# The first layer's gate in block form, the value weights' sums behind it, the turns of the next x ahead of other work

## The chip, the cores and the metric

One core of one Trainium2 chip runs the whole program. The metric is the time of one execution in microseconds (us), as the device reports it; the kernel before was run three times. A profiled execution gives start and duration of every instruction on the core's engines: TensorE (PE, with its weight loads PEld), VectorE (DVE), ScalarE (ACT), GpSimd (POOL), and the DMA queues that SyncE (SP) and POOL issue. A few matmul records are missing from a trace.

## The reference

Two layers over 512 tokens of width 1024. Each layer has a token mixer (layer 0 a Mamba-2 SSD, layer 1 an HGRN2), a squared-ReLU MLP, two layer norms, and at its end a gated per-layer input, which is what the change is about:

```python
for i in range(DEPTH):
    ...
    h = layer_norm(DEEPNORM_ALPHA * x + mix, ln_g[i, 0], ln_b[i, 0])
    h = layer_norm(DEEPNORM_ALPHA * h + sq_relu_mlp(h, mlp_w1[i], mlp_w2[i]), ln_g[i, 1], ln_b[i, 1])
    x = h + jax.nn.sigmoid(h @ ple_w_gate[i]) * (p[i] @ ple_w_proj[i])
```

`h @ ple_w_gate` is 512x1024 by 1024x1024, `p @ ple_w_proj` is 512x256 by 256x1024. After layer 0 the new x enters layer 1's mixer, whose value and output-gate projections (`v`, `g`) come first in this kernel.

## The kernel before

**Precision.** Every matmul operand is float32, split in two float32r parts, hi and lo. `mm3` (lines 119 to 122) makes one product of three matmuls: hi by hi, hi by lo, lo by hi, each 128x128 weights by 512 columns. A weight tile of 128x1024 comes by DMA into `raw` (3 buffers), ACT copies it to `whi` (line 113, 6 buffers) and DVE subtracts to make `wlo` (line 116). A new `whi` waits until PE has finished with the buffer that it takes over.

**Order.** On each engine the instructions stand in a fixed order. A scheduler makes it from the code and from priorities: work under a higher `high_priority` offset (SOON 40, EARLY 60, LEAD 100) is placed ahead of work that the code has earlier. Only in the stretches under `manual_schedule`, which begin with `values4`, does PE follow the code's own order. Each engine works through its list in order; an instruction that waits holds all behind it.

**Block form.** A product of two 2x2 block matrices may be made with seven block products in place of eight, with sums of blocks taken beforehand. `block_product` does this for the MLP, `values4` for the first value projections, `last_gate` for half of layer 1's gate. The sums of weight blocks are either made by DVE in tiles `r` (`weight_sums`, lines 322 to 345: eight loads on POOL's queue and eight subtractions or additions of 128x1024), or by DMAs that add to what lies there (`last_gate`, lines 399 to 408: a chain of eight on POOL's queue).

**Layer 0's gate before** (lines 616 to 670) is direct: for each half h of the 1024 columns and each chunk c of 128 tokens, eight `mm3` over the full depth into one PSUM bank, a sigmoid on ACT, then on DVE a product with the projection (line 664) and an addition to `acc` (line 666). While the gate runs, `transpose_split` (line 231) still turns h for its own input (PE transposes, line 238). Then `turn(h, c)` (line 620) turns each finished piece of the next x: four PE transposes into the bank `pt` (line 625), two ACT copies (lines 628, 629) and a DVE subtraction (line 630). The last turn is called in `values4` between its first and second product (lines 711, 712).

**values4** (line 672) makes layer 1's first value projections in block form from x and from the untransposed copies in `rows`. Its DVE sums of weights (`t1` to `t4`, tiles `r`) are loaded and added as early as the `r` tiles come free, which is during the last MLP product and the gate. Its products come in this order: two with plain weights, then with `t3`, `t2`, `t4`, `t1`, then one more with plain weights.

**Layer 1's gate before** is `last_gate` (line 397): 7 quarter products of 12 matmuls and 4 half products (`rest`, line 442) of 24, with `final` (line 449) doing sigmoid, product, addition and the store of the output.

Of the kernel before, what the change touches and what calls it, by code (L numbers as in the profile page):

```python
# [44 lines left out]
def trunk(ctx: ExitStack, tc, a):  # L45
# [180 lines left out]
    turned_last = []  # L226

# [57 lines left out]
    def norm(i, keep=None):  # L285
# [36 lines left out]
    def weight_sums(w, lead, after=None, queue=nc.gpsimd):  # L322
# [5 lines left out]
        def load(i, u, src):  # L328
            queue.dma_start(t[i][u], src)  # L329
# [67 lines left out]
    def last_gate(wp, wg, h_s, p_s, kept, turned):  # L397

        t3, t1, t2, t4 = (tmp("r", [P, 1024]) for _ in range(4))
        with tc.high_priority(offset=SOON):  # L400
# [7 lines left out]
            nc.gpsimd.dma_start(t4, wg[1], accum_op=ALU.add)  # L408

        pairs = [mk(b8, [P, 2, 4, 256], "b8", F32R) for _ in range(2)]  # L410
        cells = [mk(b8, [P, 4, T], "b8") for _ in range(3)] + [tmp("blk", [P, 4, T])]
        cell = lambda n: cells[n // 4][:, n % 4, :]
# [36 lines left out]
        def final(c, h, g, pp, pin=None):  # L449
# [3 lines left out]
            for ps, cs in pp:  # L453
# [5 lines left out]
                nc.sync.dma_start(a["out"][tok(c), fs], acc[:, c, fs])  # L459
# [30 lines left out]
        def put(n, f):  # L490
            t, ks = pairs[n // 2], slice(2 * (n % 2), 2 * (n % 2) + 2)
            ins = nc.scalar.copy(t[:, 0, ks, :], f)
            nc.vector.tensor_sub(t[:, 1, ks, :], f, f32(t[:, 0, ks, :]))
            return ins

        with tc.high_priority(offset=LEAD):
# [4 lines left out]
            pin = put(1, a11)  # L501
# [4 lines left out]
        raw = mk(raws, [P, 1024], "raw")  # L506
        pu = mk(w4, [P, 1024], "a", F32R), mk(w4, [P, 1024], "b", F32R)
        with tc.high_priority(offset=LEAD):
            nc.sync.dma_start(raw, wp[1])
            nc.scalar.copy(pu[0], raw)  # L510
            nc.vector.tensor_sub(pu[1], raw, f32(pu[0]))
        for n, c in enumerate((2, 3, 0)):
            ps = bank(psj, "pj")
            proj(ps, c, pu)
            nc.scalar.copy(cell(10 + n), ps)
# [11 lines left out]
        for u in range(2):  # L527
# [3 lines left out]
            final(2 + u, 0, cell(6 + u), [(cell(2 + u), whole)])  # L531
        for u in range(2):
# [25 lines left out]
    def mlp_and_gate(layer, h_s, last):  # L558
# [36 lines left out]
        for g, period in enumerate(PERIODS):  # L595
            if g < 4:
                tiles = hidden(g)
            if g > 0:
                if g == 4:
                    kept = tmp("blk", [P, 2, 4, 256]) if last else None  # L600
# [12 lines left out]
        if last:  # L613
            return last_gate(a[f"wp_{layer}"], a[f"wg_{layer}"], h_s, p_s, kept, turned)

        x_n = Split(8)
        rows = [tmp("blk", [P, 2, 4, 256]) for _ in range(2)]
        late = []

        def turn(h, c):  # L620

            sl = slice(c * P, (c + 1) * P)
            pt = bank(pst, "pt")
            for j in range(4):
                nc.tensor.transpose(pt[:, j * P : (j + 1) * P], acc[:, c, h * 512 + j * P : h * 512 + (j + 1) * P], ident)
            v = pt.rearrange("p (j t) -> p j t", j=4)
            hh = x_n.hi[h][:, :, sl]
            nc.scalar.copy(hh, v)
            nc.scalar.copy(rows[c // 2][:, h, :, c % 2 * P : (c % 2 + 1) * P], v)
            nc.vector.tensor_sub(x_n.lo[h][:, :, sl], v, f32(hh))  # L630

        pps = {}

        def proj(c, pu):

            ps = pps[c] = bank(*((psj, "pj") if c > 1 and pps else (psy, "py%d" % (c % 2))))
            sl = slice(c * P, (c + 1) * P)
            for k in range(2):
                ks = slice(k * 512, (k + 1) * 512)
                mm3(ps, p_s[0][:, k, sl], p_s[1][:, k, sl], pu[0][:, ks], pu[1][:, ks], k == 0, k == 1)  # L640

# [30 lines left out]
    def values4(xs, rows, late):  # L672
# [38 lines left out]
        for f in late:  # L711
            f()
# [751 lines left out]
```

## Time and profile before

| what | value |
|---|---|
| three runs | 1412.86, 1413.53, 1413.72 us (median 1413.53) |
| the profiled execution's own time | 1411.34 us |
| its span, first to last instruction | 1409.6 us |
| instructions | 20400 |
| DVE, ACT, POOL busy | 1069.1, 763.6, 45.8 us |
| layer 0's gate on PE | from about 699 us |
| the last turn of the next x on PE | 765.83 us |
| layer 1's gate on PE | from about 1350 us to the end |

Busy time of PE counts a matmul until its end is modelled to come, so that consecutive matmuls overlap: each 128x512 one is shown with 0.39 us, and the next starts 0.23 us after it. What PE loses must therefore be looked for in the gaps between starts and in the view of waits, not in the busy share.

### The profile page before, as it was taken

The page shows a single profiled execution, that of the slowest core. Times are in us where ns is not written, and L with a number is a line of the kernel's source. Part 1 is how long each engine was busy: PE and PEld are TensorE (multiplying, and loading weights), DVE is VectorE, ACT ScalarE, POOL GpSimd, SP SyncE. Part 2 cuts the span into 40 slices and gives each one's busy share as a digit, 9 for nine tenths or more (in the row PEclk, how much of TensorE's full clock was granted, in tenths as well). Part 3 has the DMA queues.
Part 4 walks back from the last instruction along what each step waited for, and adds up shares of the span by engine and source line. Part 5 has one row for each costly group of instructions (what it writes and reads, how often), then busy time and mean ns, then how long its engine had stood idle before and what let it go on. Part 6 is the DMA issues. An engine that isn't in the chain of part 4 may idle for free.

```text
span 1409.6 us, 20400 instructions
## 1 busy us (share of the span) xinstructions
PE 1404.3 (100%) x8001; PEld 1168.1 (83%) x8001; DVE 1069.1 (76%) x1778; ACT 763.6 (54%) x1156; POOL 45.8 (3%) x92
## 2 busy tenths in 40 slices
PE   9999999999999999999999999999999999999998
PEld 7888888888988888888888888888898888888887
DVE  7989688698977668677986577678785867667795
ACT  7766465573354444545555547655555454544573
POOL 0000000001000000000000000000100000000100
PEclk9999999999999999999999999999999999999999
DMA  8433333234433444345621421222443444444731
GB/s 313 135 117 120 106 120 110 85 100 156 141 113 127 157 131 152 129 142 178 209 90 49 134 91 61 76 87 96 150 135 105 147 137 148 144 137 159 202 106 60
DMA packets 50399, 181.69 MB, mean 129 GB/s; under 512 B 5632, under 2 KB 6400, under 8 KB 50176
## 3 DMA queue, kind: packets, MB, share of 16 engines
q1 hardware_dynamic: 38784, 138.45, 29.6%
q0 software_dynamic: 11520, 41.95, 9.2%
q8 instruction: 63, 1.03, 0.3%
q14 instruction: 32, 0.26, 0.1%
HBM read 177.16 MB, written 2.16 MB: 127 GB/s over the span
## 4 chain that ended last, share of the span: by engine, by line
PE 99%; DMA 0%; DVE 0%; issue 0%; DVEq 0%
PE pj L120 25%; PE pj L121 25%; PE pj L122 25%; PE py L120 5%; PE py L122 5%; PE py L121 5%; PE py L906 1%; PE pt L238 1%; PE py L1175 1%; PE pm L923 1%; PE pm L871 1%; PE py L1301 1%; PE pt L859 0%; PE py L1303 0%; PE py L1240 0%; PE py L832 0%
## 5 line engine op out<-in xcount | busy, mean ns | idle before, releaser
L113 ACT CAST whi<-raw 128x1024 fp32r<-128x1024 f32 x218 | 228.8, 1050 | 333.2 <-PE pj L121 243.6
L120 PE MATMUL pj<-b,whi 128*128 128x512 f32 (+1 forms) x990 | 378.6, 383 | 0.0
L122 PE MATMUL pj<-b,wlo 128*128 128x512 f32 (+1 forms) x990 | 376.8, 381 | 0.0
L121 PE MATMUL pj<-b,whi 128*128 128x512 f32 (+1 forms) x990 | 376.6, 381 | 0.0
L116 DVE TENSOR_TENSOR wlo<-raw,whi 128x1024 fp32r<-128x1024 f32 x218 | 265.4, 1221 | 129.4 <-ACT whi L113 128.2
L121 PEld LDWEIGHTS pj<-b,whi 128*128 128x128 f32 x990 | 186.4, 188 | 34.6 <-issue 0.9
L122 PEld LDWEIGHTS pj<-b,wlo 128*128 128x128 f32 x990 | 186.3, 188 | 34.5
L120 PEld LDWEIGHTS pj<-b,whi 128*128 128x128 f32 x990 | 186.1, 188 | 34.0
L122 PE MATMUL pj<-whi,b 128*128 128x512 f32 x520 | 204.1, 392 | 0.0
L120 PE MATMUL pj<-whi,b 128*128 128x512 f32 x508 | 202.1, 398 | 0.0
L121 PE MATMUL pj<-wlo,b 128*128 128x512 f32 x508 | 199.2, 392 | 0.0
L113 ACT CAST whi<-r 128x1024 fp32r<-128x1024 f32 x76 | 80.0, 1053 | 68.5 <-PE pj L122 39.4
L122 PEld LDWEIGHTS pj<-whi,b 128*128 128x128 f32 x520 | 97.7, 188 | 20.1
L120 PEld LDWEIGHTS pj<-whi,b 128*128 128x128 f32 x508 | 95.5, 188 | 19.1 <-ACT b L1322 0.3
L121 PEld LDWEIGHTS pj<-wlo,b 128*128 128x128 f32 x508 | 95.5, 188 | 18.7 <-issue 0.2
L116 DVE TENSOR_TENSOR wlo<-r,whi 128x1024 fp32r<-128x1024 f32 x76 | 92.5, 1220 | 19.6 <-ACT whi L113 19.1
L122 PE MATMUL py<-whi,b 128*128 128x512 f32 x260 | 101.3, 390 | 0.0
L121 PE MATMUL py<-wlo,b 128*128 128x512 f32 x248 | 96.6, 389 | 0.0
L120 PE MATMUL py<-whi,b 128*128 128x512 f32 x248 | 96.4, 390 | 0.0
L329 POOL DMA_DIRECT2D r<-in_w x64 | 34.0, 532 | 1098.8 <-DVE wlo L116 544.3
L122 PEld LDWEIGHTS py<-whi,b 128*128 128x128 f32 x260 | 48.8, 188 | 10.2
L800 DVE SCALAR_TENSOR_TENSOR cv<-pj,cst,cv 128x509 f32<-128x509 f32 (+2 forms) x66 | 48.9, 746 | 10.6 <-ACT cv L797 9.8
(368 smaller groups left out, 1943.5 us busy)
## 6 DMA issues: line engine op xcount, KB each, us to landing
raw<-in_w SPq DMA_DIRECT2D x112, 512.0 KB, 3.3
r<-in_w POOLq DMA_DIRECT2D x64, 512.0 KB, 3.8
raw<-in_wssd SPq DMA_DIRECT2D x36, 512.0 KB, 3.9
a<-csd SPq DMA_DIRECT2D x16, 512.0 KB, 4.1
raw<-in_wso SPq DMA_DIRECT2D x16, 512.0 KB, 3.3
raw<-in_whq SPq DMA_DIRECT2D x16, 512.0 KB, 3.4
raw<-in_wg SPq DMA_DIRECT2D x15, 512.0 KB, 4.0
raw<-in_whvg SPq DMA_DIRECT2D x14, 512.0 KB, 3.4
```

What stands on the lines that cost most here:

```text
L113: nc.scalar.copy(hi[:, :n], f)
L116: nc.vector.tensor_sub(lo[:, :n], f, f32(hi[:, :n]))
L120: nc.tensor.matmul(out, sh, mh, start=start, stop=False, **kw)
L121: nc.tensor.matmul(out, sh, ml, start=False, stop=False, **kw)
L122: return nc.tensor.matmul(out, sl, mh, start=False, stop=stop, **kw)
L238: nc.tensor.transpose(pt[:, j * P : (j + 1) * P], src[:, k * P : (k + 1) * P], ident)
L329: queue.dma_start(t[i][u], src)
L800: nc.vector.scalar_tensor_tensor(cv[:, d:], ps[:, : T - d], convw[:, i, k : k + 1], cv[:, d:], ALU.mult, ALU.add)
L871: nc.tensor.matmul(pst_[:, c * P : (c + 1) * P], btok[:, c, :], xw[:, c].rearrange("p h q -> p (h q)"), start=True, stop=True)
L906: mm = nc.tensor.matmul(yds[0][64 * r : 64 * r + 64, sl], xdt[:, 2 * c + r, :], m[:, r, sl], start=True, stop=True)
L923: mm = nc.tensor.matmul(yo[:, c * P : (c + 1) * P], pv[:, c - 1].rearrange("p h q -> p (h q)"), cm[:, c * P : (c + 1) * P], start=True, st ...
L1175: nc.tensor.matmul(pcs[r][bs, at : at + n], kk[r][:, ts], qs, start=True, stop=True)
```

## The change

Layer 0's gate takes the form of layer 1's. `last_gate` becomes `block_gate` with a flag `last`, and the direct form, its `proj` and its `turn` are gone. For layer 0 the block form differs from layer 1's in these points:

- the projections of the second half (`wp[1]`) are made next to the chunk that uses them, not early;
- there are fewer SBUF tiles for partial results (`cells`, `homes`), and nothing is stored to the output;
- `turn` is called at eight places, two of them (`turn(1, 0)` and `turn(1, 1)`) inside `values4`: one before the second chunk of its first product, one after that product;
- `turn` has its ACT and DVE work under LEAD, and takes the bank `pm` for even chunks and `pt` for odd ones;
- the loads of `weight_sums` for the values are placed behind the last DMA of the gate's chain (`added`) on POOL's queue, its DVE sums behind the gate's last sum of h (`summed_last`) in DVE's list.

Besides, the layer norm ahead of layer 0's gate has the priority SOON for its last two chunks too (before 0), and h keeps an untransposed copy (`kept`) in layer 0 as in layer 1.

```diff
@@ norm
-            with tc.high_priority(offset=LEAD if c == 3 and i % 2 == 0 else 0 if c > 1 and i == 1 else SOON):
+            with tc.high_priority(offset=LEAD if c == 3 and i % 2 == 0 else SOON):
@@ weight_sums
-    def weight_sums(w, lead, after=None, queue=nc.gpsimd):
+    def weight_sums(w, lead, after=None, held=None):
         def load(i, u, src):
-            queue.dma_start(t[i][u], src)
+            with behind(held):
+                nc.gpsimd.dma_start(t[i][u], src)
@@ last_gate, now block_gate
-            nc.gpsimd.dma_start(t4, wg[1], accum_op=ALU.add)
+            added = nc.gpsimd.dma_start(t4, wg[1], accum_op=ALU.add)
+        if last:
+            cells = [mk(b8, [P, 4, T], "b8") for _ in range(3)] + [tmp("blk", [P, 4, T])]
+            cell = lambda n: cells[n // 4][:, n % 4, :]
+        else:
+            cells = [mk(b8, [P, 4, T], "b8"), tmp("blk", [P, 4, T])]
+            homes = [(0, 0), (0, 1), (0, 2), (0, 3), (1, 0), (1, 1), (0, 0), (0, 1), (1, 2), (1, 3)]
+            cell = lambda n: cells[homes[n][0]][:, homes[n][1], :]
-            put(3, a12)
+            summed_last = put(3, a12)[1]
+        gate_last[:] = summed_last, added
...
+        x_n = Split(0)
+        rows = [None, None]
+        def turn(h, c):
...
+            pt = bank(pst, "pt") if c % 2 else bank(psm, "pm")
+            for j in range(4):
+                nc.tensor.transpose(pt[:, j * P : (j + 1) * P], acc[:, c, h * 512 + j * P : h * 512 + (j + 1) * P], ident)
...
+            with tc.high_priority(offset=LEAD):
+                nc.scalar.copy(hh, v)
+                nc.scalar.copy(rows[c // 2][:, h, :, c % 2 * P : (c % 2 + 1) * P], v)
+                nc.vector.tensor_sub(x_n.lo[h][:, :, tok(c)], v, f32(hh))
         for u in range(2):
+            if not last and u:
+                turn(0, 2)
             part(x[u], summed(2), t1, u, False)
             nc.vector.tensor_add(cell(8 + u), x[u], cell(8 + u))
         us = [negated(wg[6]), negated(wg[7])]
         b22 = unit(wg[5])
+        if not last:
+            pu = unit(wp[1])
+            for u in range(2):
+                g = bank(psj, "pj")
+                rest(g, 2 + u, us, True)
+                nc.vector.tensor_add(cell(8 + u), g, cell(8 + u))
+                ps = bank(psj, "pj")
+                proj(ps, 2 + u, pu)
+                final(2 + u, 1, cell(8 + u), [(ps, whole)])
+                if u == 0:
+                    turn(0, 3)
+            for u in range(2):
+                part(x[u], summed(3), b22, u, False, False)
+                if u:
+                    turn(0, 1)
+                rest(x[u], u, us, False)
+                if u == 0:
+                    turn(0, 0)
+                ps = bank(psj, "pj")
+                proj(ps, u, pu)
+                final(u, 1, x[u], [(ps, whole)])
+                turn(1, 2 + u)
+            return x_n, rows, [lambda: turn(1, 0), lambda: turn(1, 1)]
@@ mlp_and_gate: the direct form goes
-        if last:
-            return last_gate(a[f"wp_{layer}"], a[f"wg_{layer}"], h_s, p_s, kept, turned)
...
-                for k in range(8):
-                    ks = slice((k % 2) * 512, (k % 2 + 1) * 512)
-                    mm3(pg, h_s.h(k, sl), h_s.l(k, sl), gu[k // 2][0][:, ks], gu[k // 2][1][:, ks], k == 0, k == 7)
...
+        return block_gate(a[f"wp_{layer}"], a[f"wg_{layer}"], h_s, p_s, kept, turned, last)
@@ values4
-        t1, t2, t3, t4 = weight_sums(w, VALUE_SUMS)
+        t1, t2, t3, t4 = weight_sums(w, VALUE_SUMS, *gate_last)
         def product(x, us, banks, start, drain):
             for c in range(2):
+                if late and c:
+                    late.pop(0)()
         product(part(0, 0), [unit(v) for v in w[0][0]], x, True, first(0, 0))
-        for f in late:
-            f()
+        late.pop(0)()
         product(part(0, 1), [unit(v) for v in w[1][0]], z, True, more(0, 0))
```

How the lists of the engines move, at three places. A row names the line, the operation, the tile written and the tiles read, the size, and the engines or DMA queues that it waits for.

**The eight sums of the value weights on DVE.** Before, they stand during the last MLP product and the first half of the gate; the last four of them (tiles `r`, lines 339 to 344) stand among the gate's own products and additions (lines 664, 666) and the splits of h (line 243):

```order
L339 TENSOR_TENSOR r_6348<-r_6348,r_6344 128x1024 [waits DMASW5_49]
L664 TENSOR_TENSOR sg_5966<-py_1021_5923,sg_5966 128x512 [waits Activation_49]
L243 TENSOR_TENSOR b_921_5529<-pt_5992,b_919_5527 128x4x128 [waits Activation_49]
L666 TENSOR_TENSOR acc_99<-sg_5966,acc_99 128x512 [waits DVE_49]
L340 TENSOR_TENSOR r_6344<-r_6342,r_6344 128x1024
L243 TENSOR_TENSOR b_920_5528<-pt_6019,b_918_5526 128x4x128 [waits Activation_49]
L344 TENSOR_TENSOR r_6345<-r_6345,r_6343 128x1024 [waits DMASW6_49]
```

Now six of the eight stand in the last third of the gate, where line 573 adds a half product, line 463 multiplies by the projection, line 465 adds to `acc` and line 559 is the subtraction of a turn:

```order
L573 TENSOR_TENSOR blk_5904<-pj_6262,blk_5904 128x512 [waits PE_49]
L342 TENSOR_TENSOR r_6384<-r_6382,r_6384 128x1024
L463 TENSOR_TENSOR sg_6283<-pj_6276,sg_6283 128x512 [waits PE_49,Activation_49]
L338 TENSOR_TENSOR r_6383<-r_6383,r_6389 128x1024 [waits DMASW4_49,DMASW3_49]
L465 TENSOR_TENSOR acc_99<-sg_6283,acc_99 128x512 [waits DVE_49]
L341 TENSOR_TENSOR r_6389<-r_6389,r_6385 128x1024 [waits DMASW5_49,DVE_49]
L346 TENSOR_TENSOR r_6386<-r_6386,r_6384 128x1024 [waits DMASW6_49]
L342 TENSOR_TENSOR r_6385<-r_6383,r_6385 128x1024 [waits DVE_49]
L559 TENSOR_TENSOR b_1053_6188<-pm_6306,b_1052_6187 128x4x128 [waits PE_49,Activation_49]
L346 TENSOR_TENSOR r_6387<-r_6387,r_6385 128x1024 [waits DMASW7_49,DVE_49]
L463 TENSOR_TENSOR sg_6321<-pj_6314,sg_6321 128x512 [waits PE_49]
```

The sums have moved from ahead of and beside the gate's first half to just ahead of the last chunks' additions to `acc`.

**The last addition to acc ahead of the last turn, on DVE.** Before, it is line 666 on `sg_6303`, and it stands ahead of the two weight splits (line 116) of tiles `r_6343` and `r_6344`, the sum t2:

```order
L664 TENSOR_TENSOR sg_6303<-py_1069_6295,sg_6303 128x512 [waits Activation_49]
L630 TENSOR_TENSOR b_1003_5890<-pt_6331,b_1001_5888 128x4x128 [waits PE_49,Activation_49]
L666 TENSOR_TENSOR acc_99<-sg_6303,acc_99 128x512 [waits DVE_49]
L1016 CAST lmask_6658<-raw_6659 128x256 [waits DMAHW0_49]
L116 TENSOR_TENSOR wlo_6507<-r_6343,whi_6505 128x1024 [waits Activation_49]
L116 TENSOR_TENSOR wlo_6511<-r_6344,whi_6509 128x1024 [waits PE_49,Activation_49]
L630 TENSOR_TENSOR b_1003_5890<-pt_6417,b_1001_5888 128x4x128 [waits PE_49,Activation_49]
```

Now it is line 465 on `sg_6368`, and it stands behind the same two splits (tiles `r_6384`, `r_6385`), its product (line 463) and a sum of x (line 712):

```order
L116 TENSOR_TENSOR wlo_6556<-r_6384,whi_6554 128x1024 [waits Activation_49]
L116 TENSOR_TENSOR wlo_6560<-r_6385,whi_6558 128x1024 [waits Activation_49]
L463 TENSOR_TENSOR sg_6368<-pj_6361,sg_6368 128x512
L712 TENSOR_TENSOR blk_6189<-blk_6189 128x1024
L465 TENSOR_TENSOR acc_99<-sg_6368,acc_99 128x512 [waits DVE_49]
L713 TENSOR_TENSOR blk_6189<-blk_6189,blk_6305 128x1024 [waits DVE_49]
L1014 CAST lmask_6707<-raw_6708 128x256 [waits DMAHW7_49]
L679 TENSOR_TENSOR b_1119_6514<-blk_6189,b_1119_6514 128x1024 [waits Activation_49]
L559 TENSOR_TENSOR b_1080_6326<-pt_6466,b_1079_6325 128x4x128 [waits PE_49,Activation_49]
```

The addition that the last turn reads has passed from ahead of the splits of t2 to behind them.

**The last turn on PE.** It stands at the same place as before, after the last matmul of `values4`'s first product; now with these rows:

```order
L121 MATMUL py_1099_6411<-wlo_6430,b_1052_6187 128x512
L122 MATMUL py_1099_6411<-whi_6428,b_1053_6188 128x512
L553 MATMUL pt_6466<-cst_165,acc_99 128x128 [waits DVE_49,PE_49]
L553 MATMUL pt_6466<-cst_165,acc_99 128x128 x3
L120 MATMUL pj_6412<-whi_6476,b_1079_6325 128x512 [waits Activation_49]
```

`whi_6558`, which the second split on DVE reads, takes over the buffer of `whi_6428`; the matmul of the second row here is the last one that uses it.

More of the change, by code (lines that the diff above doesn't have):

```diff
@@ L226, in trunk @@
     turned_last = []
+    gate_last = []
     def behind(ins):
@@ L599, in mlp_and_gate @@
                 if g == 4:
-                    kept = tmp("blk", [P, 2, 4, 256]) if last else None
+                    kept = tmp("blk", [P, 2, 4, 256])
                     h_s, after, turned, sums = norm(2 * layer + 1, kept)
```

86 lines of the change are left out of this document (23 added, 63 removed).

## The prediction

> **What bounds the kernel now.** I read the page first, then the view of PE's waits, then the busy time by stage. The page:
>
> ```profile
> span 1409.6 us, 20400 instructions
> PE 1404.3 (100%) x8001; PEld 1168.1 (83%) x8001; DVE 1069.1 (76%) x1778; ACT 763.6 (54%) x1156; POOL 45.8 (3%) x92
> PE 99%; DMA 0%; DVE 0%; issue 0%; DVEq 0%
> ```
>
> The chain that ended last is PE for 99% of the span. Whether PE ever stood still is told by its waits over the whole execution:
>
> ```profile
> PE pm L153 <- PEq L1452: 0.8, 1, 0.8
> PE py L749 <- DVE b L167: 0.6, 1, 0.6
> ```
>
> There are two, both in the first microseconds, 1.4 us together. So the program lasts as long as PE's list of matmuls, and a change can act in two ways only: by the number of matmuls, or by a wait that PE does not have now. Which engine could make PE wait around layer 0's gate is seen by stage (columns: stretch, then busy us of PE, PEld, DVE, ACT, POOL with instructions, granted clock, DMA share, GB/s; the fourth is in layer 1's gate, which already has the block form):
>
> ```profile
> 699.00:727.00 28.00, 28.00 (x143) 23.12 (x142) 25.62 (x39) 14.63 (x28) 0.00 (x0) 1.00 0.20 67
> 727.00:757.00 30.00, 30.00 (x141) 24.80 (x140) 16.72 (x21) 13.23 (x19) 0.00 (x0) 1.00 0.22 71
> 757.00:772.00 15.00, 15.00 (x71) 12.17 (x70) 12.44 (x14) 9.87 (x14) 0.00 (x0) 1.00 0.35 115
> 1355.00:1376.00 21.00, 21.00 (x103) 17.30 (x102) 20.29 (x28) 16.63 (x30) 0.00 (x0) 1.00 0.20 67
> ```
>
> The reader is to see that DVE is nearly full at the start of either gate (25.6 of 28 us, 20.3 of 21 us), and has room from 727 to 757 us (16.7 of 30). That room is where the change puts more work. The third view is the timeline around the last turn of the next x, where PE meets what DVE made last. Its rows give all durations that I need:
>
> ```profile
> 763.42 0.69 DVE L666 TENSOR_TENSOR acc<-sg,acc 128x512 f32<-128x512 f32 x1
> ...
> 765.60 0.39 PE L122 MATMUL py<-whi,b 128*128 128x512 f32 x1
> 765.83 0.60 PE L625 MATMUL pt<-cst,acc 128*128 128x128 f32 x4
> 766.19 0.48 PE L120 MATMUL pj<-whi,b 128*128 128x512 f32 x1
> 766.50 0.40 PE L121 MATMUL pj<-wlo,b 128*128 128x512 f32 x1
> 766.51 1.05 ACT L113 CAST whi<-r 128x1024 fp32r<-128x1024 f32 x1
> ...
> 767.60 1.23 DVE L116 TENSOR_TENSOR wlo<-r,whi 128x1024 fp32r<-128x1024 f32 x1 [0.58 <-ACT whi L113]
> 768.74 0.69 DVE L630 TENSOR_TENSOR b<-pt,b 128x512 fp32r<-128x512 f32 x1
> 769.34 0.68 DVE L702 TENSOR_TENSOR a<-pj,a 128x512 f32<-128x512 f32 x1
> 769.94 1.22 DVE L714 TENSOR_TENSOR blk<-blk 128x1024 f32<-128x1024 f32 x1
> 770.17 0.39 PE L122 MATMUL pj<-whi,b 128*128 128x512 f32 x1
> 770.39 0.39 PE L120 MATMUL pj<-whi,b 128*128 128x512 f32 x1
> 770.59 1.06 ACT L113 CAST whi<-r 128x1024 fp32r<-128x1024 f32 x1 [2.06 <-PE pj L122]
> 771.19 1.23 DVE L715 TENSOR_TENSOR blk<-blk,blk 128x1024 f32<-128x1024 f32 x1
> ```
>
> A matmul starts 0.23 us after the one ahead (770.17, 770.39) and ends 0.39 us after its start. Four transposes cost 0.36 us and make the next gap 0.31 instead of 0.23: 0.44 in all. An ACT copy of a weight tile that waits for its buffer starts 0.03 us after the end of the last matmul on it (770.17 + 0.39, 770.59) and takes 1.05. DVE's split follows 0.04 us later (766.51 + 1.05, 767.60). On a busy DVE, one row of 1024 columns puts the next 1.14 us later (767.60, 768.74), one of 512 columns 0.60 (768.74, 769.34); a single result is ready after 1.22 or 0.69. And the addition to `acc` that the last turn reads was ready at 764.11, 1.7 us ahead of the turn at 765.83. That is the margin today.
>
> **The change part by part.**
>
> *Fewer matmuls.* The direct gate is 2 halves x 4 chunks x 8 mm3 = 64 mm3, 192 matmuls. The block form is 7 quarter products of 4 mm3 and 4 half products of 8 mm3 = 60 mm3, 180 matmuls. Projections (16 mm3) and turns (8 x 4 transposes) are as many as before. 12 matmuls fewer x 0.227 us = **-2.7 us**, and that is all that can be gained.
>
> *The sums of the gate's weights by DMA.* Eight more DMAs on POOL's queue, in a chain where each addition waits for what it adds to, and the values' loads now stand behind them there. Layer 1's gate shows the same chain and its last user, and the present loads and sums of the values stand in the view of the tiles r from 650 to 730 us:
>
> ```profile
> 1304.75 0.53 POOL L401 DMA_DIRECT2D r<-in_wg  x1 [20.86 <-DVE wlo L116]
> 1333.24 0.86 POOL L408 DMA_DIRECT2D r<-in_wg  x1 [5.57 <-DMA r<-r]
> 1372.57 1.22 DVE L116 TENSOR_TENSOR wlo<-r,whi 128x1024 fp32r<-128x1024 f32 x1
> ```
>
> ```profile
> L329 POOL DMA_DIRECT2D r<-in_whvg x8: 527/530/537, 653.4 to 675.0; - x8
> L336 DVE TENSOR_TENSOR r<-r,r x2: 1220/1220/1220, 680.5 to 681.6; 128x1024 f32<-128x1024 f32 x2
> L344 DVE TENSOR_TENSOR r<-r,r x2: 1218/1221/1224, 718.5 to 721.5; 128x1024 f32<-128x1024 f32 x2
> DMA to landing us min/median/max: 3.6/3.8/4.8
> ```
>
> The gates lie about 651 us apart (first gate load here at 1304.75, first value load at 653.4, both when the same r tile comes free), so in layer 0 the chain runs from about 653 to 682 us. Four of the eight values' loads then find tiles free; the others wait for the gate's own splits, the last at 1372.57 - 651 = 721 us, and land within 5 us, by 727. The sums that need them stand far back in DVE's list and run after about 742 us (below), so these loads cost **0**; were the 15 us of cover gone, each late load would hold DVE for up to 4.8 us.
>
> *More on DVE.* In the order, from the last half product added to `acc`'s second half (line 573) to the row ahead of t2's splits, DVE has 22 rows: 12 of 1024 columns, six of them value sums, and 10 of 512. That is 12 x 1.14 + 10 x 0.60 = 19.7 us. In the same stretch PE has 78 matmuls and five turns, 78 x 0.227 + 5 x 0.44 = 19.9 us. The two run level: DVE has neither margin nor a large debt when PE reaches the last turn. I take **0.3 us** of debt; the ends are 0 and 1.2 (one wide row).
>
> *The last turn waits for what cannot be made earlier.* This is the term that decides. PE's last turn reads `acc` after the addition of line 465, which on DVE stands behind both splits of t2. The second split reads `whi_6558`, whose ACT copy waits for the last matmul on `whi_6428`, and this matmul is the one directly ahead of the turn on PE. So PE stands still for the whole loop. Without a wait the turn would come at 765.83 - 2.72 = 763.1, the matmul ahead of it starting at 762.9. Step by step: its end, 763.27; ACT copy from 763.30 to 764.35; split on DVE from 764.39; its product (line 463) at 765.53; the wide sum (line 712) at 766.13; the addition (line 465) from 767.27 to 767.96; the turn, with a weight load of its own, at about 768.1. **+5.0 us**, in place of the present margin of 1.7. Everything behind the turn on PE's list is moved by it. Queued behind the addition on DVE are line 713, a small cast, the split of line 679 (which needs ACT's copy, 1.05 us, after line 713) and then the turn's own subtraction, which the third matmul of the second product's second chunk needs: 767.9 + 1.22 + 1.05 + 1.14 + 0.69 = 772.0 against 768.1 + 0.44 + 12 x 0.227 + 0.45 = 771.7, with the weight load **+0.5 us** (ends 0 and 1).
>
> *The other turns.* Six turns in the gate wait for additions to `acc` in the same way, but with no loop through PE; counted along DVE's list they come within half a microsecond of their need. I take **+0.1**, ends 0 and 1. The ACT copies of `kept` and of the cells (some 20 of about 0.6 us) lie in ACT's idle time: 13.2 of 30 us are used. Elsewhere in the program the lists are the same but for names.
>
> The sum: -2.7 + 5.0 + 0.3 + 0.5 + 0.1 = **+3.2 us**. Against the profiled execution that is 1409.6 + 3.2 = 1412.8 us of span, with 1.7 us around it as now (1411.34 - 1409.6) 1414.5. The median of the runs lies 2.2 us above that execution: 1413.53 + 3.2 = **1416.7 us**. With the ends of the terms the forecast's own range is -2.7 + 5.0 = +2.3 to -2.7 + 5.0 + 1.2 + 1 + 1 = +5.5: 1415.8 to 1419.0.
>
> **The rivals.**
>
> *PE's clock falls in the wait.* The granted clock is 1.00 in every row above, but PE nowhere stands still for more than 0.8 us, so the trace cannot show what 5 us do. After the 0.6 us wait of line 749 the next matmuls follow at the usual spacing. If the clock fell, the product behind the turn, 24 matmuls of 0.227 = 5.4 us, would be slower in part; all of it at half speed is the upper end, +5.4, a quarter of it +1.4. I take +1.4: 1418.1.
> [...]
>
> *The wait is not there, or short: not slower.* If the buffer of `whi_6558` came free before the first product ends, or the addition were ready while DVE still has margin, the turn would meet its rows as it does today, and only the 12 matmuls would count, with the 0.5 behind: 1413.53 - 2.7 + 0.5 = 1411.3. It decides as soon as the addition is ready by 763. For it: the margin today is 1.7 us with the same splits nearby. Against it: today's addition stands ahead of those splits, and the rows at 766.51 and 770.59 show ACT copying right behind PE's last use.
>
> *DVE falls behind earlier.* If its 1024-column rows run later than counted, say because a raw weight tile lands late, the turns of the gate's last third wait too, each for 0.3 to 0.6 us, four of them, +2: 1418.7. For it: DVE and PE run level there. Against: layer 1's gate keeps PE without a wait with DVE busy in 20.3 of 21 us.
>
> **How the numbers follow.** Forecast 0.5, the clock 0.2, the short wait 0.2, DVE behind 0.1. A measurement of this kernel can tell about 0.2%, 2.8 us, from no change: faster is below 1410.7, slower above 1416.4. The forecast lies just above that bound, so of its 0.5 about 0.35 are slower and 0.15 same; the clock and the late DVE are slower (0.3); of the short wait 0.04 are faster, 0.16 same. Together: slower 0.65, same 0.31, faster 0.04. The range reaches over the clock's case and below the forecast's own low end, 1414.0 to 1419.2; most of the short wait's chance is left out below.
>
> **What would show it.** In the profile of the changed kernel: 12 matmuls fewer; one wait of PE at line 553 on DVE (line 465) of about 5 us, at about 763 us, and one of about half a microsecond behind it; ACT's copy directly behind the last matmul ahead of the wait, then DVE without a gap until line 465. Wrong would be: no such wait, waits spread over several turns, a DMA as the releaser, or a clock below 1.00 behind the wait.

## The result, and the profile after

The changed kernel takes 1421.04 us (median of 6 runs, 1418.69 to 1422.47) against 1412.92 us of the kernel before (6 runs, 1411.61 to 1413.72): ratio 1.0056, 95% interval 1.0043 to 1.0069, or 6.1 to 9.7 us more. It is slower, as predicted, but by 8.1 us where 3.2 were forecast, and outside the range (1414.0 to 1419.2).

The profiled execution has a span of 1418.0 us, 8.4 more than before. Its page and the view of PE's waits (us in total, times, longest):

```profile
span 1418.0 us, 20428 instructions
PE 1405.6 (99%) x7989; PEld 1167.5 (82%) x7989; DVE 1081.3 (76%) x1797; ACT 775.0 (55%) x1177; POOL 51.5 (4%) x100
PE 95%; DVE 3%; DMA 1%; ACT 0%; issue 0%; DVEq 0%; ACTq 0%
```

```profile
PE pt L553 <- DVE acc L465: 4.9, 1, 4.9
PE pt L239 <- DVE acc L224: 2.2, 2, 1.6
```

12 matmuls fewer, and yet PE is busy 1.3 us longer: some of them took longer than before. Two waits of more than 0.3 us are new. The one at line 553, the last turn, was predicted; the one at line 239, the transposes of h behind the layer norm ahead of the gate (`transpose_split`; line 224 is the norm's last row), was not. The timeline around the last turn:

```profile
765.38 0.39 PE L122 MATMUL py<-whi,b 128*128 128x512 f32 x1
765.81 1.04 ACT L113 CAST whi<-r 128x1024 fp32r<-128x1024 f32 x1 [0.33 <-PE py L122]
765.85 2.35 DVE L116 TENSOR_TENSOR wlo<-r,whi 128x1024 fp32r<-128x1024 f32 x2
768.12 0.68 DVE L463 TENSOR_TENSOR sg<-pj,sg 128x512 f32<-128x512 f32 x1
768.72 1.22 DVE L712 TENSOR_TENSOR blk<-blk 128x1024 f32<-128x1024 f32 x1
769.85 0.68 DVE L465 TENSOR_TENSOR acc<-sg,acc 128x512 f32<-128x512 f32 x1
770.68 1.08 PE L553 MATMUL pt<-cst,acc 128*128 128x128 f32 x4 [4.91 <-DVE acc L465]
771.42 0.77 PE L120 MATMUL pj<-whi,b 128*128 128x512 f32 x1
771.99 0.63 PE L121 MATMUL pj<-wlo,b 128*128 128x512 f32 x1
772.42 0.63 PE L122 MATMUL pj<-whi,b 128*128 128x512 f32 x1
```

The predicted steps are there: ACT's copy starts 0.04 us after the end of the matmul (765.38 + 0.39), DVE then runs without a gap through the second split, lines 463, 712 and 465, and PE stands still until 770.68. From start to start, 765.38 to 770.68, that is 5.30 us instead of 0.23. But DVE has no gap ahead of the second split either. The pair of splits takes 2.35 us and one alone 1.22, so the second starts at 766.98: 0.13 us after the end of ACT's copy (765.81 + 1.04), where a split that waits for its copy follows 0.04 us behind. So the loop through PE and DVE's own list end within 0.1 us of each other, and DVE's list is the later one. Behind the turn the matmuls follow 0.43 us apart (771.99, 772.42), where the spacing was 0.23. The busy time in stretches that end where the clock changes shows why (stretch and its length, busy us of PE, PEld, DVE, ACT, POOL; granted clock, DMA share, GB/s):

```profile
765.82:769.24 3.42, 0.00 (x0) 0.00 (x0) 3.42 (x5) 1.52 (x2) 0.00 (x0) 1.00 0.00 0
769.24:772.65 3.41, 1.97 (x7) 1.80 (x8) 2.64 (x4) 0.89 (x1) 0.00 (x0) 0.50 0.02 5
772.65:776.07 3.42, 3.42 (x9) 2.64 (x9) 2.96 (x3) 2.26 (x5) 0.00 (x0) 0.50 0.45 153
776.07:779.50 3.43, 3.43 (x16) 2.79 (x16) 2.88 (x4) 2.03 (x3) 0.91 (x2) 1.00 0.00 0
```

The granted clock fell to 0.50 at 769.24 us, during the wait, and stayed there for 6.8 us. The second new wait begins around the DMAs on POOL's queue. The rows around it, the two queues' loads from 670 to 700 us after the change and the same of before (KB each, median us to landing), and the chain to PE:

```profile
679.08 0.88 POOL L410 DMA_DIRECT2D r<-in_wg  x1 [3.05 <-DMA r<-r]
679.65 2.47 POOL L331 DMA_DIRECT2D r<-in_whvg  x4
...
688.71 1.05 ACT L113 CAST whi<-raw 128x1024 fp32r<-128x1024 f32 x1 [1.15 <-DMA raw<-in_wp]
696.89 2.46 DVE L224 SCALAR_TENSOR_TENSOR acc<-acc,lnrs,b 128x1024 f32<-128x1024 f32 x2
698.21 0.66 PE L239 MATMUL pt<-cst,acc 128*128 128x128 f32 x4 [1.61 <-DVE acc L224]
```

```profile
r<-in_whvg POOLq DMA_DIRECT2D x4, 512.0 KB, 13.7
raw<-in_wp SPq DMA_DIRECT2D x1, 512.0 KB, 8.7
```

```profile
r<-in_whvg POOLq DMA_DIRECT2D x4, 512.0 KB, 4.4
raw<-in_wp SPq DMA_DIRECT2D x2, 512.0 KB, 4.3
```

As soon as the hold of the change ends, behind the gate's last summing DMA (line 410), four loads of value weights go out in one burst, since four tiles are free. The raw weight tile of wp, issued on SP's queue 0.9 us after that last summing DMA, lands 8.7 us after its issue; the same load took 5.2 us before (issued at 679.37; 4.3 is the median of two). The next raw tile, of wg, takes 7.1 us instead of 3.2. Their splits (line 116) come late on DVE, the layer norm behind them too, and PE waits 1.6 us at line 239.

**Where the 8.4 us lie.** DVE's row of `lnsum` in the MLP marks the same work in both kernels (line 373 before, 375 after), in layer 0 and layer 1:

```profile
679.85 0.68 DVE L373 CUSTOM_DVE_ANT_0 acc<-pj,acc 128x512 f32<-128x512 f32 x1
1331.22 0.68 DVE L373 CUSTOM_DVE_ANT_0 acc<-pj,acc 128x512 f32<-128x512 f32 x1
```

```profile
680.43 0.68 DVE L375 CUSTOM_DVE_ANT_0 acc<-pj,acc 128x512 f32<-128x512 f32 x1
1338.66 0.68 DVE L375 CUSTOM_DVE_ANT_0 acc<-pj,acc 128x512 f32<-128x512 f32 x1
```

| stretch | us | from |
|---|---|---|
| ahead of layer 0's gate | +0.6 | 680.43 - 679.85; such a shift differs between executions: the wp load below, at 679.4 us before, goes out at 679.5 and 679.1 in experiments 11 and 12 |
| gate, 12 matmuls fewer | -2.7 | 8001 - 7989, x 0.227 |
| gate, line 239 | +1.8 | the gap with the wait, 2.00 instead of 0.23 |
| gate, last turn | +5.1 | 5.30 - 0.23 |
| behind it, half clock | +2.6 | turn to next matmul 0.74 for 0.36; the next gap 0.57 for 0.31; ten gaps from 771.99 to 776.18, 4.19 for 2.27 |
| layer 1, line 239 again | +0.6 | the second of its two waits |
| rest | +0.4 | not assigned |

From mark to mark it is (1338.66 - 680.43) - (1331.22 - 679.85) = +6.9 us, of which the four middle rows make 6.8. The 0.6 us in layer 1 is in this execution only by chance: it is 0.3 or absent in most executions of the kernels below, and 0.8 in one that does not have the change at all.

### The profile page after: what moved, and what is told of

Read it like the earlier page. It is cut to its first block, busy times and chain, and to the rows that moved or that the text cites. A ratio compares the mean times of both kernels' runs of the same rounds, so it can differ in the third digit from the quotient of the medians.

```text
span 1418.0 us, 20428 instructions
## 1 busy us (share of the span) xinstructions
PE 1405.6 (99%) x7989; PEld 1167.5 (82%) x7989; DVE 1081.3 (76%) x1797; ACT 775.0 (55%) x1177; POOL 51.5 (4%) x100
## 4 chain that ended last, share of the span: by engine, by line
PE 95%; DVE 3%; DMA 1%; ACT 0%; issue 0%; DVEq 0%; ACTq 0%
PE pj L120 24%; PE pj L121 24%; PE pj L122 24%; PE py L122 5%; PE py L120 5%; PE py L121 5%; PE py L904 1%; DVE wlo L116 1%; PE pt L239 1%; PE py L1173 1%; PE pm L869 1%; PE pm L921 1%; DMA acc<-in_x 1%; PE py L1299 1%; DVE cv L798 0%; PE pt L857 0%
## 5 line engine op out<-in xcount | busy, mean ns | idle before, releaser
L116 DVE TENSOR_TENSOR wlo<-raw,whi 128x1024 fp32r<-128x1024 f32 x215 | 261.9, 1221 | 134.1 <-ACT whi L113 133.4
L122 PE MATMUL pj<-whi,b 128*128 128x512 f32 x504 | 198.5, 394 | 0.0
L120 PE MATMUL pj<-whi,b 128*128 128x512 f32 x480 | 192.3, 401 | 0.0
L121 PE MATMUL pj<-wlo,b 128*128 128x512 f32 x480 | 189.0, 394 | 0.0
L113 ACT CAST whi<-r 128x1024 fp32r<-128x1024 f32 x80 | 84.2, 1054 | 67.3 <-PE pj L122 38.3
L116 DVE TENSOR_TENSOR wlo<-r,whi 128x1024 fp32r<-128x1024 f32 x80 | 97.3, 1219 | 20.8 <-ACT whi L113 20.5
L122 PEld LDWEIGHTS pj<-whi,b 128*128 128x128 f32 x504 | 95.2, 189 | 19.8
L121 PE MATMUL py<-wlo,b 128*128 128x512 f32 x272 | 106.1, 390 | 0.0
L122 PE MATMUL py<-whi,b 128*128 128x512 f32 x272 | 105.9, 389 | 0.0
L120 PE MATMUL py<-whi,b 128*128 128x512 f32 x272 | 105.9, 391 | 0.0
L120 PEld LDWEIGHTS pj<-whi,b 128*128 128x128 f32 x480 | 90.8, 189 | 18.2 <-ACT b L1320 0.3
L121 PEld LDWEIGHTS pj<-wlo,b 128*128 128x128 f32 x480 | 90.8, 189 | 17.8 <-issue 0.2
L120 PEld LDWEIGHTS py<-whi,b 128*128 128x128 f32 x272 | 51.1, 188 | 10.7
L122 PEld LDWEIGHTS py<-whi,b 128*128 128x128 f32 x272 | 51.1, 188 | 10.6
```

Source lines behind the costliest of these rows:

```text
L113: nc.scalar.copy(hi[:, :n], f)
L116: nc.vector.tensor_sub(lo[:, :n], f, f32(hi[:, :n]))
L120: nc.tensor.matmul(out, sh, mh, start=start, stop=False, **kw)
L121: nc.tensor.matmul(out, sh, ml, start=False, stop=False, **kw)
L122: return nc.tensor.matmul(out, sl, mh, start=False, stop=stop, **kw)
```

## The experiments

Each ratio is to the kernel before on the same chip (medians 1412.62, 1411.99 and 1412.23 us in the three comparisons). The edits are against the changed kernel, in the last two against the kernel before.

**1. The turns without their priority.**

```diff
-            with tc.high_priority(offset=LEAD):
+            with tc.high_priority(offset=0):
                 nc.scalar.copy(hh, v)
```

> The changed kernel, with the copies and the subtraction of the turns of the next x back at priority 0. DVE's addition to acc for the last turn (line 465) then stands ahead of both splits of t2. Theory (PE stands still because that addition stands behind splits that wait for PE itself): PE's wait at line 553 falls from 4.9 to under 0.7 us, the granted clock stays 1.00, PE's wait at line 239 stays near 1.6; 1421.0 - 4.9 - 2.6 = about 1413.5 us. Rival (DVE simply has too much work in the gate, and whatever stands last is late): the waits only move to other matmuls of the second product, 4 us or more in all, 1419 us or more.

1413.72 us, ratio 1.0009 (1.0000 to 1.0018). In the order the addition to `acc` now stands ahead of both splits of t2, and the waits are:

```profile
PE pt L239 <- DVE acc L224: 1.7, 1, 1.7
PE pt L553 <- DVE b L559: 1.4, 1, 1.4
```

The 4.9 us are gone, the clock is 1.00, and 7 of the 8 us are back. What is left at line 553 is at the turn ahead of the last one, a wait for the bank's earlier subtraction (line 559), which has lost its priority. So the last turn's wait comes from one part of the change, the priority of the turns' copies and subtractions: it puts the last addition behind the splits.

**2. The loads' hold moved to the last sum of the gate's rows (`summed_last`), in the order alone.**

```diff
-        gate_last[:] = summed_last, added
+        gate_last[:] = summed_last, summed_last
```

> The changed kernel, with the values' eight weight loads held until the gate's blocks are summed (some 35 us later), and nothing else; DVE's order of rows is the same. Theory (four of these loads, issued within 2.5 us at 680 us, delay the raw weight tile of wp, DVE's split of it and the layer norm behind it): that tile lands within 5 us instead of 8.7, PE's wait at line 239 in layer 0 falls from 1.6 to under 0.3 us, line 553 stays at 4.9: 1421.0 - 1.6 = 1419.4 us. Rival (the wait at line 239 comes from the order of DVE's rows): it stays at 1.6, 1421.0 us.

1423.81 us, 1.0080 (1.0068 to 1.0092): worse, and the line-239 wait grew from 1.6 to 3.2 us. The edit did not do what it was made for. It fixes the order of issue only, no engine waits for the other, and on the chip two of the loads went out ahead of the gate's last summing DMA, two behind it:

```profile
676.69 1.08 POOL L331 DMA_DIRECT2D r<-in_whvg  x2
682.07 0.89 POOL L410 DMA_DIRECT2D r<-in_wg  x1 [4.30 <-DMA r<-r]
682.63 1.41 POOL L331 DMA_DIRECT2D r<-in_whvg  x2
686.38 1.05 ACT L113 CAST whi<-raw 128x1024 fp32r<-128x1024 f32 x1 [3.97 <-DMA raw<-in_w]
```

It tells something all the same: DVE's rows there are those of the changed kernel, and the wait doubled. It follows the traffic on POOL's queue, not the order of DVE's rows. But the gate's last summing DMA moved too, from 679.1 to 682.1 us, so it does not tell the loads from that DMA. The clock falls behind this wait as well (at half from 698.3 to 705.1 us).

**3. The addition early: product and addition of the last two chunks with the priority LEAD.** (4 is the same with the edit of 2.)

```diff
+                with tc.high_priority(offset=LEAD) if h and c < 2 and not last else nullcontext():
+                    nc.vector.tensor_mul(sg[:, cs], ps[:, cs], sg[:, cs])
+                    nc.vector.tensor_add(acc[:, c, fs], sg[:, cs], acc[:, c, fs])
```

> The changed kernel, with the product and the addition to acc of the last two gate pieces that the turns read (second half, chunks 0 and 1) at a priority of 100; the turns keep theirs. Theory: as in the run without the turns' priority: no wait over 0.7 us at line 554, clock 1.00, line 239 still 1.6, 1413.5 us. Rival (too much DVE work): waits of 4 us or more in other places, 1419 us or more.

> Both edits: the early addition and the later loads. Theory: neither wait is left, 1421.0 - 4.9 - 2.6 - 1.6 = 1411.9 us, about 1 us below the kernel before (12 matmuls fewer are worth 2.7, about 1 goes to small waits). Rival: the two waits share a cause, the gain is less than their sum, 1414 us or more.

1418.78 us, 1.0046 (1.0034 to 1.0059), and 1418.77 us, 1.0049 (1.0037 to 1.0061). The wait at line 553 is gone in both, but another has taken its place. Of the first:

```profile
PE py L120 <- ACT b L679: 3.2, 1, 3.2
PE pt L239 <- DVE acc L224: 1.5, 1, 1.5
```

DVE is full there: from 761.68 to 782.11 us it stands idle once, for 0.79 us. With the addition ahead, the sums of x (lines 713, 714) stand behind the splits, ACT's copy of the fourth product's block (line 679) is late, and PE waits 3.2 us for it. In both that wait is followed by a fall of the clock, in 4 though PE was busy for 1.39 of the 3.41 us ahead of the fall:

```profile
779.53:782.94 3.41, 1.39 (x5) 0.87 (x6) 3.40 (x4) 3.35 (x5) 0.00 (x0) 0.99 0.00 1
782.94:786.35 3.41, 3.41 (x10) 2.63 (x9) 1.57 (x2) 0.00 (x0) 1.28 (x4) 0.51 0.00 0
```

**5. The loads made to wait on the chip for the gate's last sums,** by a DVE memset of one column in each of their first four tiles, ordered behind those sums. **6** is 5 with the edit of 1.

```diff
+            for i, u in ((0, 0), (2, 0), (1, 0), (0, 1)) if held is not None else ():
+                with behind(after), tc.high_priority(offset=400):
+                    nc.vector.memset(t[i][u][:, 0:1], 0.0)
```

> The changed kernel, with four DVE writes of one column (128x1) into the values' first four load tiles, placed behind the sums of the gate's blocks; so the four loads that went out at 680 us wait on the chip until about 725 us (in the run with the loads 'held' later they had not waited: that edit orders the issue only, and two loads went out even earlier, at 676.7). DVE's rows up to there are the same. Theory (the burst of loads delays wp's raw tile, its split and the layer norm): wp's tile lands within 5 us, PE's wait at line 239 in layer 0 under 0.3 us, line 556 stays at 4.9 with the clock behind it: 1421.0 - 1.6 = 1419.4 us. Rival (the order of DVE's rows): 1.6 us stays, 1421 us.

> The waiting loads and the turns at priority 0 together. Theory: 1413.7 (turns at priority 0) - 1.65 (line 239) = 1412.1 us, no wait of PE over 1.5 us, clock 1.00. Rival (the late loads make DVE's sums late): a new wait, 1414 us or more.

1422.59 us, 1.0075 (1.0062 to 1.0088), and 1416.78 us, 1.0034 (1.0021 to 1.0046). The loads' issue and PE's waits in the first of the two:

```profile
725.58 4.59 POOL L331 DMA_DIRECT2D r<-in_whvg  x8 [42.24 <-ACT blk L535]
```

```profile
PE pt L556 <- DVE acc L468: 5.2, 1, 5.2
PE pm L556 <- DVE b L562: 2.3, 1, 2.3
PE pm L556 <- DVE acc L468: 0.9, 1, 0.9
```

In 5, without the burst, the wp tile lands 5.6 us after its issue and line 239 has no wait at all. In 6 the burst is gone too, and yet the wp tile takes 8.5 us, as in the changed kernel; the wait is 0.5 us. So the burst alone does not make the wp tile late. The loads are now too late for the sums, which crowd into the gate's last third and delay three turns (line 556 here): this way of moving the loads costs more than it saves. The wait at the last turn also grows here, from 4.9 to 5.2 us, with DVE's list some 0.4 us behind the loop.

**7. The value loads and sums not held, as before the change.**

```diff
-        t1, t2, t3, t4 = weight_sums(w, VALUE_SUMS, *gate_last)
+        t1, t2, t3, t4 = weight_sums(w, VALUE_SUMS)
```

> The changed kernel without the hold: the values' loads and sums have no order against the gate's sums, as in the kernel before. Theory: two of the loads go out ahead of the gate's last addition by DMA, and three value sums that need them stand on DVE ahead of wp's split; the wait at line 239 grows to 3 us or more; the addition for the last turn stands between the two splits of t2, so line 553 waits 2 to 4 us; 1419 to 1424 us. Rival (the hold is what costs, by pressing DVE's sums into the gate's last third): 1416 us or less.

1425.51 us, 1.0096 (1.0081 to 1.0112), the slowest of all and above the expected 1424. PE waits 4.2 us at line 239, 2.1 us for an `lnsum` row, 1.7 us at line 553, and twice under 1 us; the wp tile lands after 10.3 us, and the sums hold up DVE:

```profile
DVE r L338 <- DMA r<-in_whvg: 4.9, 1, 4.9
DVE r L341 <- DMA r<-in_whvg: 3.9, 1, 3.9
```

The hold is thus a part of the change that helps: without it the loads meet the gate's DMAs earlier (two of them go out at 676.15 us, where the first goes out at 679.65 with the hold), and the sums hold up DVE.

**8. The layer norm's priority as before the change.**

```diff
-            with tc.high_priority(offset=LEAD if c == 3 and i % 2 == 0 else SOON):
+            with tc.high_priority(offset=LEAD if c == 3 and i % 2 == 0 else 0 if c > 1 and i == 1 else SOON):
```

> The changed kernel with the layer norm's priority of chunks 2 and 3 as before the change. The addition for the last turn then stands between the two splits of t2, not behind both. Theory (what stands ahead of the addition on DVE sets the wait): line 553 waits 2 to 3.7 us instead of 4.9, line 239 stays at 1.6 or so; 1417 to 1420 us. Rival (the place in the list does not matter, DVE's total does): 4.9 us stays, 1421 us.

1416.07 us, 1.0032 (1.0021 to 1.0044).

```profile
PE pt L239 <- DVE acc L224: 2.6, 1, 2.6
PE pt L553 <- DVE acc L465: 1.7, 1, 1.7
PE pj L121 <- DVE wlo L434: 1.1, 1, 1.1
```

The waits are moved and split: the addition now stands between the two splits of t2. Together with a last one of 0.2 us they are 5.6 us, only 0.9 less than the 6.5 us of the changed kernel's gate, yet the kernel is 4 us faster against its kernel before (+4.1 instead of +8.1). The clock stays at 1.00 here (in the profiled execution; the slowest run, of 1419.4 us, has 0.997), so by this difference some 3 us of the 8.1 are the clock's.

**9. POOL's queue made to wait for the layer norm** (a one-column copy ahead of the value loads), which leaves DVE's rows as they are. **10** is 9 with the edit of 1.

```diff
+        with behind(added):
+            added = nc.gpsimd.tensor_copy(mk(sm, [P, 1], "lnrs"), acc[:, 1, 0:1])
```

> The changed kernel with one POOL copy of a single column (128x1) of acc's chunk 1, behind the gate's last addition by DMA: POOL's queue, and the values' first four loads in it, then wait on the chip until the layer norm of chunk 1 is done (about 699 us), not until 725 as in the run with DVE's writes. DVE's rows are the same as in the changed kernel. Theory (burst of loads): wp's raw tile lands within 6 us, line 239 waits under 0.5 us in layer 0, no new wait of DVE for the values' loads, line 555 stays at 4.9 with the clock behind it; 1421.0 - 1.6 = 1419.4 us. Rival (the order of rows): 1.6 us stays, 1421 us.

> The same POOL copy, and the turns at priority 0. Theory: neither of the two waits is left in full: PE waits under 0.5 us at line 239 and about 1.4 at line 555, clock 1.00; -2.7 + 1.4 + 0.5 = about 0.8 us below the kernel before in the same comparison. Rival (a third limit): a new wait of over 1 us, time not below the kernel before.

1417.07 us, 1.0037 (1.0024 to 1.0049), and 1412.07 us, 1.0002 (0.9993 to 1.0011). In 9 PE still waits 4.9 us at the last turn. The loads go out at 709.87 us, the wp tile lands after 5.4 us, and of the line-239 wait 1.3 us are left, this time with a raw tile of wg that is late; in 10 there is none. In 10 PE waits once:

```profile
PE pt L555 <- DVE b L561: 1.4, 1, 1.4
```

It is the wait that experiment 1 left. With both new waits gone and the clock at 1.00 the kernel is back at the time of the one before. The 2.7 us of the fewer matmuls should leave it 1.3 us faster after this wait; the interval (-1.0 to +1.6 us) just misses that. From mark to mark its profiled execution takes 1331.38 - 680.82 = 650.56 us, 0.8 less than before, so that with a wait of 1.4 some 2.2 of the 2.7 are seen. No version here is measurably faster than the kernel before.

**What line 239 waits for.** The traces of these runs hold the issue and the landing of each DMA (us; ahead and behind are against the issue of the wp load):

| kernel | the gate's last summing DMA | value loads nearby | wp lands after | next wg tile after | wait at 239 |
|---|---|---|---|---|---|
| changed | 0.9 ahead | four, from 0.3 ahead | 8.7 | 7.1 | 1.6 |
| 2 | 2.4 behind | two from 2.9 ahead, two from 3.0 behind | 9.7 | 8.7 | 3.2 |
| 5 | 2.2 behind | none | 5.6 | 5.2 | none |
| 6 | 0.9 ahead | none | 8.5 | 5.5 | 0.5 |
| 9 | 2.0 behind | none | 5.4 | 6.8 | 1.3 |
| 10 | 0.4 behind | none | 5.1 | 4.9 | none |

DVE's rows up to the layer norm are the same in all six. On DVE the wp tile's split stands ahead of the wg tile's, and this one ahead of the norm's last rows. From the mark of above to the wg tile's split it is 11.9 us in the changed kernel and 10.8 in 6. A late wp tile needs no burst: in 6 the gate's own last summing DMA stands alone ahead of it. The burst shows in the wg tile, 7.1 against 5.5 us, and there the waits differ by 1.1. But 9, without a burst, has a late wg tile too.

**11 and 12. The kernel before, with a wait of PE alone:** four, or eight, extra DVE rows ahead of the addition that the last turn reads.

```diff
+                with tc.high_priority(offset=LEAD):
+                    for _ in range(4 if h == 1 and c == 3 else 0):
+                        nc.vector.scalar_tensor_tensor(sg, sg, 0.0, sg, ALU.mult, ALU.add)
                 nc.vector.tensor_add(d, sg, d)
```

Each row adds zero times `sg` to `sg`, so the values stay as they are.

> The kernel before, with four more DVE instructions (sg*0 + sg, 128x512) ahead of the addition that the last turn reads, and nothing else: PE waits about 2.6 us at the turn. Theory (a wait well under 3.4 us leaves the clock): clock 1.00, 2.6 us over the kernel before. Rival (any wait costs the clock too): 4 us or more over it.

> The same with eight such instructions: PE waits about 6.2 us at the turn. Theory: the granted clock falls to half in or behind the wait for one to three stretches of 3.41 us, and the time is 8 to 10 us over the kernel before. Rival (a wait costs its own length): 6.2 us over it, clock 1.00.

Eight rows: 1421.97 us, 1.0068 (1.0055 to 1.0080), +9.7 us for a wait of 6.4, with the clock at half for 6.8 us, from within the wait on. Four rows: 1416.18 us, 1.0028 (1.0017 to 1.0038), +3.9 us for a wait of 2.5. The wait, and in stretches of 3.41 us the clock, of the four rows:

```profile
PE pt L625 <- DVE acc L669: 2.5, 1, 2.5
```

```profile
766.51:769.92 3.41, 1.02 (x7) 0.96 (x8) 3.34 (x4) 1.81 (x3) 0.00 (x0) 1.00 0.27 105
769.92:773.33 3.41, 3.41 (x10) 2.64 (x9) 1.82 (x2) 0.72 (x2) 0.00 (x0) 0.50 0.00 0
```

The clock fell after a wait of 2.5 us too; the theory that under 3.4 us it stays up has fallen. It does not fall each time: the two fastest runs of this kernel (1414.9 us) have a mean clock of 1.000. In a kernel without the change, the waits cost 1.4 and 3.3 us more than they last; the profiled executions have one more wait each that is not in the kernel before, of 0.8 and 1.0 us, so that not all of it need be the clock. An estimate from the traces: PE works for 3.4 us (four rows) and 5.0 us (eight rows, 773.50 to 778.54) at half clock, and half of that, 1.7 and 2.5 us, is lost.

## Where the prediction held and where it failed

*Fewer matmuls, -2.7.* Right in number (8001 to 7989). No run measures the 2.7 by itself; experiment 10 shows some 2.2 of it in its trace.

*The last turn, +5.0.* Right in place, releaser, order and size (5.07 in the trace). Experiments 1 and 8 show that it hangs on where the addition stands among the splits of t2, and that the turns' priority, with the layer norm's, put it there. That the loop through PE makes the wait is not shown: DVE's list alone ends 0.1 us later than the loop, in experiment 5 some 0.4 us later, and no run takes the loop away (with one more buffer for `whi`, say). That both come to the same size here is partly luck.

*The debt of DVE, the second wait, the other turns, +0.9 together.* Of the debt 0.1 us is seen, inside the long wait; the other two are not seen as waits. The second wait is absent with the clock at half behind the turn: the twelve matmuls that were to take 2.7 us took nearly twice that (771.42 to 776.42, 5.0 us), and the subtraction of line 559 came in time.

*The first step that failed: the clock, left to a rival with a chance of 0.2 and a price of 1.4.* The prediction said that the trace of before could not show what a wait of 5 us does, and then chose the case without an effect for its forecast. The profiled execution lost 2.6 us. Over the six runs the mean clock is 0.996 to 0.999, and the slower ones have the lower clock (1422 us at 0.996, 1419 us at 0.998 and 0.999); runs of the kernel before, in the three comparisons, have 0.999 at the least. Experiment 12 shows the same without the change.
The traces show the clock at half for 3.41 us (experiments 4 and 11) or 6.8 us (the changed kernel, experiment 12), with the matmuls 0.43 us apart. In the changed kernel PE was idle in the whole step ahead of the fall (765.82 to 769.24, no matmul), but elsewhere the clock fell after steps in which PE was busy for 1.02 and 1.39 us of 3.41 (experiments 11 and 4). An estimate from these: a wait of 4.9 us that lies half in one step and half in the next leaves 3.41 - 2.45 = 0.96 us of work in each, less than in steps after which the clock fell. So by these traces a wait of 4.9 us would cost the clock wherever it lies.

*The second step that failed: the sums of the gate's weights by DMA and the value loads behind them, "these loads cost 0".* The prediction asked who waits for the value loads (nobody, with 15 us of cover; that held) and not what else is under way while the DMAs of POOL's queue land. The raw tiles of wp and wg on SP's queue landed late (8.7 and 7.1 us instead of 5.2 and 3.2), and they lead through their splits and the layer norm to PE: +1.8 us. Which DMA of POOL's queue delays them is open in part. With the value loads later, line 239 still waited 1.3 us in experiment 9 and 0.5 in 6, and not at all in 5 and 10. Experiment 6 speaks for the gate's own last summing DMA as the cause of the late wp tile, and for the burst as the cause of some 1.1 us through the wg tile; experiment 9 has the late wg tile without the burst. No run moved the summing DMA on purpose.

*The rival "DVE falls behind earlier"* was near to this in its cause (a raw tile that lands late) but named the wrong place: not the turns of the gate's last third, but the layer norm ahead of the gate. *The short wait* needed the addition ahead of t2's splits, which is what experiment 1 brings about; its time of 1413.7 us against the rival's 1411.3 differs by the wait at line 239 and one that the lost priority makes.

So the sum would have come out with two terms changed: -2.7 + 5.1 + 2.6 + 1.8 = +6.8, against +6.9 from mark to mark. The rest of the 8.4 us lies ahead of the gate and in layer 1, where nothing that recurs was found.

## What to carry to other kernels

On a kernel that keeps PE full, count with more than the length of a wait of PE: here waits of 2.5, 4.9 and 6.4 us (experiment 11, the changed kernel, experiment 12) cost, besides what they last, some 1 to 3 us by a slower clock (each left a step of 3.41 us with 1.4 us of work or less). Several shorter waits can be cheaper than one long one: those of experiment 8, 5.6 us together and none above 2.6, left the clock up in the profiled execution, and that kernel was 4 us faster than the changed one with its 6.5. When a change puts more DMAs on a queue, ask not only who waits for them but which transfers on other queues will land late beside them (here the wp tile, after 8.7 us instead of 5.2). On an engine without room, a row that is moved ahead moves another one back (experiment 3: the wait of 4.9 us gone, one of 3.2 us in its place), and an order of issue is not a wait on the chip (experiment 2: two of the loads went out at 676.69 us, ahead of the gate's last summing DMA at 682.07).

## What the runs showed of the hardware

- In these traces the granted clock falls to 0.50 and rises again in steps of 3.41 us, for one of them (769.92 to 773.33 in experiment 11) or two (769.24 to 776.07 in the changed kernel); at half clock matmuls of 512 columns follow 0.427 us apart (771.99 to 775.83 in the changed kernel, 3.84 us for nine gaps), at full clock 0.227.
- PE was not idle for the whole of each step ahead of a fall. Counted from the start of the first record of the granted clock (1.00), the steps run on through a whole execution: in the changed kernel that record starts at 4.66 us, and the fall at 769.24 us comes 764.59 us, 224 steps of 3.413, behind it; in the kernel before it starts at 3.60 us, and a fall behind the last matmuls, at 1409.89 us, comes 412 steps later. In the 14 traces of this case every step at full clock with 1.43 us of PE work or less is followed by half clock (13 times, the ends of the executions not counted), and none with 1.63 us or more is. The two nearest to the bound, of experiments 2 and 7, and behind the second one more that falls:

```profile
694.86:698.27 3.41, 1.43 (x7) 0.85 (x5) 3.41 (x10) 3.21 (x8) 0.00 (x0) 1.00 0.69 233
700.02:703.44 3.42, 1.63 (x7) 0.96 (x6) 2.56 (x9) 3.42 (x10) 0.00 (x0) 1.00 0.61 198
703.44:706.85 3.41, 0.99 (x7) 0.90 (x8) 3.41 (x4) 2.69 (x5) 0.00 (x0) 1.00 0.00 0
```

- So where a wait lies within the steps decides. In experiment 8 the wait of 2.6 us lay across two steps and left 2.19 and 2.04 us of work in them, that of 1.7 us left 2.47 and 2.65, and the clock stayed up. No run set this on purpose. Runs of the same changed kernel spread over 3.8 us, in the order of their mean clock.
- Four loads of 512 KB issued together on POOL's queue took 13.7 us (median) to land (4.4 for the four of the same stretch before the change, issued 1.3 to 1.7 us apart). A single load on SP's queue took 8.7 us beside them, and 8.5 us without them but 0.9 us behind a summing DMA on POOL's queue; it took 5.1 to 5.6 us where that DMA was issued behind it and no value load was near.
